# One flag of the framework: instructions ordered by its second machine model

## The chip, the cores and the metric

The kernel runs on one core of a Trainium2 chip. The core has five engines with an instruction stream each: TensorE (PE, matmuls, with the weight load shown apart as PEld), VectorE (DVE), ScalarE (ACT), GpSimd (POOL) and SyncE (SP, which issues most DMAs). An engine takes its instructions in the order in which the program has them; between engines, semaphores make an instruction wait for another's result. The metric is the time of one execution on the device in microseconds, the median of several runs.

## The reference

One inference step of a small decoder: two layers, a prompt group of 1024 tokens and a sample group of 8 sequences with one new token each, which share all weights. Layer 0 mixes with a gated linear recurrence (HGRN2), layer 1 with stick-breaking attention over one shared K/V; both layers also attend to 256 memory tokens, and both have a SwiGLU FFN. All inputs are float32.

```python
for l in range(DEPTH):
    hn = rmsnorm(h, g[0])
    if l < N_A:
        mix, S = a_mixer(hn, ...)          # HGRN2 recurrence and memory attention
    else:
        mix = b_mixer(hn, ...)             # stick-breaking over k_all, v_all and memory attention
    h = h + rmsnorm(mix, g[1])
    h = h + rmsnorm(swiglu(rmsnorm(h, g[2]), w_gu[l], w_down[l]), g[3])
    if l == N_A - 1:
        sb_k, sb_v = jnp.split(rmsnorm(h, g_kv) @ w_kv, 2, axis=-1)
```

For the sample group, attention reads caches: shared K/V in pages that a page table names (2 pages of 128 positions for each of the 8 sequences), and memory K/V of 256 tokens for each layer and sequence.

## The kernel before, in words

Tokens are on the free axis, features on the partitions. The prompt is cut into two groups of 512 tokens; group 1 carries the 8 sample tokens too, so its tiles are 520 wide and its matmuls go in two pieces of 260 columns, those of group 0 in one of 512.

**Projections.** All large products go through `proj` (L255 to L268). `split_w` loads 4 blocks of 128 x 128 weights in one DMA on SP's queue (L245), ScalarE rounds them to the fast float32 format of TensorE (L250), and VectorE forms the rest (L251); activations are split the same way (L271, L272). Each block then takes three matmuls (L264): high by high, high by low, low by high. The sums go into one of two PSUM accumulators (`mmp`, 2 buffers, tag `mm`); a third tile can start only when one has been evacuated (L403 on VectorE for the down projection, L281 and L474 for the FFN's gate and up, and others).

**Streams that are woven.** The kernel is written as generators; `weave` takes turns between streams in the order in which the program is written. Near the end it reads:

```python
weave((chain(b1.sb(), b1.mem()), 40), (chain(f0.part(0), f0.part(1)), 18))
weave((chain(b1.sb_sample(), b1.mem_sample()), 40), (chain(f0.part(2), f0.part(3)), 16))
o1 = out_proj(1, 1, A, True)
drain(o1.mm(b1.xo))
```

So layer 1's stick-breaking (`sb_prompt`, L1048 to L1075) and memory attention (`mem_attn`, L632 to L663) of the second group are written between the parts 0 and 1 of the first group's FFN, the sample group's two attentions between the parts 2 and 3, and the output projection behind both.

**The sample group's attention.** `sample_scores` puts the query in rows (transposes L679, copy L681), stores it to DRAM (L683) and loads it for each sequence to all partitions (L689). Then for each of 8 sequences it takes a tile of keys, 128 x 2 x 512, multiplies by the query (L690) and sums (L691), both on VectorE. `sample_pv` weights a tile of values (L702, in place), adds its two halves (L703), and TensorE sums over the partitions (L704); L707, L710, L271 and L272 put the result into the tiles `xo` that the output projection reads. The tiles `c` come from a pool of 4 buffers: in stick-breaking by gathers on POOL's queue (L731, two for each sequence), in memory attention by plain DMAs on SP's (L719). Between scores and weighting stand, in stick-breaking, L1084, a softplus (L1024 to L1027), three small matmuls (L1088 to L1090) and L1091, and in memory attention transposes (L745), a softmax (L747 to L752) and transposes back (L755).

**What sets the order.** The code above is only traced: the framework's `TileContext` collects the instructions with their dependences and priorities (the order written), and when the context closes, a scheduler plays them on a model of the machine. An instruction whose inputs are there and whose engine is free in the model is sent out, the earliest written first; the order in which they were sent is the order of each engine's stream, and is fixed. Buffers of a pool are handed out in the same run. A few copies are written for any engine (`nc.any.tensor_copy`, L777 and in `store_y`), and the scheduler picks the engine. The flag of the change stands in the last lines of `kernel`, where the context is opened.

Lines used below beside these: L293 to L295 (sum of squares over the partitions, and the reciprocal root), L304 (adding up squares), L310 (the normed residual), L384 to L390 (the residual itself), L846 and L849 (the recurrence for the sample group), L999 (evacuation of the shared K/V projection), L775 (transposes of the v projection).

## Time and profile before

| what | us |
|---|---|
| median of 3 runs | 2555.13 (2554.44 to 2561.5) |
| the profiled execution | 2559.18 |
| its span, first to last instruction | 2557.5 |
| TensorE busy in it | 2526.6 |
| mean granted TensorE clock in it | 0.992 |

The profile shows one execution. Rows of groups give line, engine, operation, output and inputs, shapes and count; behind the first bar the busy time of all in us and the mean of one in ns, behind the second the idle time of the engine just before them and what ended it. Rows of the timeline begin with the start in us and the duration, then engine, line and operation; a wait before the instruction stands in square brackets with what ended it. Matmuls of one run are merged into one row; a matmul in plain float32 can show as two records. Numbers of buffers are left out of the names.

### The profile page before, as it was taken

The numbers are of one execution on the slowest core, as the hardware profiler recorded it, in microseconds if no ns is written. First come the engines' busy times: TensorE is split into PE (matmuls) and PEld (weight loads), VectorE is DVE, ScalarE is ACT, GpSimd is POOL, SyncE is SP. The second block draws the span as 40 slices with busy tenths as digits, with TensorE's granted clock in tenths as the row PEclk, the third lists the DMA queues.
The fourth block names the chain that finished last, engine by engine and source line by source line (L and its number), as shares of the span: only waits on it lengthen the run. The fifth ranks groups of instructions, "written<-read, shape, count | busy, mean of one in ns | idle before, by whom it ended". The sixth has DMA issues, their size and how long they took to land.

```text
span 2557.5 us, 40523 instructions
## 1 busy us (share of the span) xinstructions
PE 2526.6 (99%) x15649; PEld 2205.3 (86%) x15649; DVE 1555.5 (61%) x2709; ACT 1183.6 (46%) x2186; POOL 40.7 (2%) x59
## 2 busy tenths in 40 slices
PE   8999999999999999999999999999999999999998
PEld 6888898888867888999999989867776798999998
DVE  6666566654675576555544576666678758444445
ACT  6346543243434455555433454566543245443334
POOL 1000000000000000000000000000021000000000
PEclk9999999998999999999999999999999999999999
DMA  6352242233563445322333446322157544333332
GB/s 183 110 161 71 73 150 77 65 111 110 158 182 91 128 153 178 103 86 60 97 94 92 125 146 189 113 82 75 46 175 217 156 125 125 111 88 100 95 92 67
DMA packets 457708, 297.91 MB, mean 116 GB/s; under 512 B 17573, under 2 KB 422642, under 8 KB 457514
## 3 DMA queue, kind: packets, MB, share of 16 engines
q1 hardware_dynamic: 454954, 286.92, 37.4%
q0 software_dynamic: 2560, 8.39, 1.1%
q8 instruction: 123, 2.02, 0.3%
q14 instruction: 71, 0.58, 0.1%
HBM read 265.44 MB, written 29.80 MB: 115 GB/s over the span
## 4 chain that ended last, share of the span: by engine, by line
issue 25%; PE 22%; DVE 1%; POOL 1%; DMA 1%; ACT 0%; DVEq 0%; POOLq 0%; SPq 0%; ACTq 0%
PE mm L264 21%; POOL c L731 1%; PE s L704 0%; DMA w<-in_w_gu 0%; DMA b<-qd 0%; DMA c<-in_cache_sb_v,pidx 0%; PE s L1125 0%; DVE c L690 0%; DVE sc L691 0%; PE ns L293 0%; PE s L440 0%; DVE yT L542 0%; DVE c L702 0%; PE s L508 0%; DVE yT L539 0%
## 5 line engine op out<-in xcount | busy, mean ns | idle before, releaser
L264 PE MATMUL mm<-x,ws 128*128 128x260 f32 (+1 forms) x10080 | 1676.5, 324 | 6.0 <-DVE ws L251 3.1
L264 PEld LDWEIGHTS mm<-x,ws 128*128 128x128 f32 x10080 | 1452.6, 189 | 167.4 <-issue 24.6
L250 ACT CAST ws<-w 128x512 fp32r<-128x512 f32 (+1 forms) x800 | 475.6, 595 | 911.9 <-PE mm L264 816.7
L251 DVE TENSOR_TENSOR ws<-w,ws 128x512 fp32r<-128x512 f32 (+1 forms) x800 | 522.2, 658 | 346.6 <-ACT ws L250 336.7
L264 PE MATMUL mm<-m,ws 128*128 128x260 f32 (+1 forms) x3168 | 542.6, 325 | 1.1 <-DVE t L474 0.5
L264 PEld LDWEIGHTS mm<-m,ws 128*128 128x128 f32 x3168 | 453.4, 188 | 59.8 <-issue 15.3
L403 DVE TENSOR_TENSOR r<-r,mm 128x520 f32<-128x520 f32 (+1 forms) x128 | 88.3, 690 | 88.9 <-PE mm L264 87.8
L281 DVE TENSOR_SCALAR t<-mm 128x512 f32<-128x512 f32 (+1 forms) x104 | 72.2, 694 | 110.2 <-PE mm L264 109.0
L474 DVE TENSOR_TENSOR t<-t,mm 128x512 f32<-128x512 f32 (+1 forms) x88 | 60.8, 691 | 116.1 <-PE mm L264 116.0
L285 DVE TENSOR_TENSOR t<-t,t 128x512 f32<-128x512 f32 (+1 forms) x88 | 61.1, 695 | 84.9 <-ACT t L284 84.8
L304 DVE TENSOR_TENSOR st<-st,n 128x512 f32<-128x512 f32 (+1 forms) x98 | 67.1, 691 | 6.9 <-ACT n L303 5.0
L272 DVE TENSOR_TENSOR m<-t,m 128x512 fp32r<-128x512 f32 (+1 forms) x88 | 61.0, 693 | 3.5 <-ACT m L271 1.6
L282 ACT ACTIVATE t<-t 128x512 f32<-128x512 f32 (+1 forms) x88 | 55.9, 635 | 12.1 <-DVE t L281 4.6
L271 ACT CAST m<-t 128x512 fp32r<-128x512 f32 (+1 forms) x88 | 54.9, 623 | 13.9 <-DVE t L474 6.9
L283 ACT ACTIVATE t<-t 128x512 f32<-128x512 f32 (+1 forms) x88 | 55.9, 635 | 2.6
L284 ACT ACTIVATE t<-t 128x512 f32<-128x512 f32 (+1 forms) x88 | 55.9, 635 | 2.3
L892 PEld LDWEIGHTS s<-a,a 128*128 128x128 f32 x448 | 53.4, 192 | 1.2
L892 PE MATMUL s<-a,a 128*128 128x64 f32 x448 | 53.1, 271 | 0.0
L731 POOL DMA_INDIRECT c<-in_cache_sb_k,pidx x16 | 16.6, 1038 | 1874.7 <-DVE r L403 1247.9
L1027 DVE SCALAR_TENSOR_TENSOR b<-b,b 128x512 f32<-128x512 f32 (+3 forms) x48 | 26.8, 558 | 29.7 <-ACT b L1026 29.3
L643 ACT ACTIVATE b<-s,nmx 128x256 f32<-128x256 f32 x64 | 29.8, 470 | 28.7 <-DVE nmx L637 28.7
L1075 PE MATMUL s<-b,a 128*128 128x512 f32 (+3 forms) x96 | 41.5, 514 | 0.3
(293 smaller groups left out, 1948.0 us busy)
## 6 DMA issues: line engine op xcount, KB each, us to landing
w<-in_w_gu SPq DMA_DIRECT2D x352, 256.0 KB
w<-in_w_down SPq DMA_DIRECT2D x160, 256.0 KB
w<-in_w_in_a SPq DMA_DIRECT2D x80, 256.0 KB
w<-in_w_o SPq DMA_DIRECT2D x64, 256.0 KB
w<-in_w_mem_kv SPq DMA_DIRECT2D x32, 256.0 KB
c<-in_cache_mem_k SPq DMA_DIRECT2D x16, 512.0 KB
c<-in_cache_mem_v SPq DMA_DIRECT2D x16, 512.0 KB
w<-in_w_kv SPq DMA_DIRECT2D x32, 256.0 KB
```

Source lines behind the costliest of these rows:

```text
L250: nc.scalar.copy(ws[:, 0, :n, :], raw[:, :n, :])
L251: nc.vector.tensor_sub(ws[:, 1, :n, :], raw[:, :n, :], ws[:, 0, :n, :].bitcast(F32))
L264: nc.tensor.matmul(ps[:, a, : PW[g]], wt, xt[k][:, xi, o : o + PW[g]], start=(k == 0 and wi == 0), stop=(k == nk - 1 and wi == 2),)
L272: nc.vector.tensor_sub(dst[1], src, dst[0].bitcast(F32))
L281: nc.vector.tensor_scalar(sv(x, g), pv(ps, g), -44.0, None, op0=ALU.max)
L282: nc.scalar.activation(d, x[:, :n], AF.Exp, scale=-1.0)
L283: nc.scalar.activation(d, d, AF.Ln, bias=1.0)
L285: nc.vector.tensor_mul(d, d, x[:, :n])
L304: nc.vector.tensor_add(acc[:, :n], acc[:, :n], t[:, :n])
L403: nc.vector.tensor_add(dst, dst, pv(ps, g))
L474: nc.vector.tensor_mul(sv(sg, g), sv(sg, g), pv(pu, g))
L892: nc.tensor.matmul(plv[:, hh, c, :], K_[:, hh, cs], rhs, start=True, stop=True)
```

## The change

The context is opened with the flag `schedule_with_timeline_sim`: the scheduler plays the instructions on the framework's second machine model, one of device occupancy, in place of its first. Nothing of the traced program changes: the same operations, tiles, pools and dependences go in.

```diff
--- before.py
+++ after.py
@@ -1221,7 +1221,7 @@
         args.append(nc.dram_tensor(f"in_{name}", a.shape, mybir.dt.from_np(a.dtype), kind="ExternalInput").ap())
     for name, shape in _OUTS:
         args.append(nc.dram_tensor(f"out_{name}", shape, F32, kind="ExternalOutput").ap())
-    with tile.TileContext(nc) as tc:
+    with tile.TileContext(nc, schedule_with_timeline_sim=True) as tc:
         tile_decoder(tc, *args)
     r = run_bass_kernel_spmd(nc, [arrays], core_ids=[0])
     return tuple(r.results[0][f"out_{name}"] for name, _ in _OUTS)
```

In the built program each engine has the same number of matmuls, vector operations and DMAs as before, but for seven of the copies for any engine, which are now on ScalarE and were on VectorE, and some 40 more instructions that only wait. The order differs on all engines. Around the sample group's attention in layer 1, TensorE's stream now reads (buffer numbers kept):

```
L264 Matmult mm_19059<-m_18847,ws_19056 128x512 x3
L264 Matmult mm_19088<-x_15705,ws_19080 128x260
L264 Matmult mm_19149<-x_15705,ws_19141 128x260
L1088 Matmult s_18243<-ss_18238,trif 128x32
L1089 Matmult s_18243<-ss_18238,ones 128x32
L1090 Matmult s_18243<-ss_18238,trif 128x32
L704 Matmult s_18249<-c_18250,sel 8x512
...
L704 Matmult s_18249<-c_18406,sel 8x512
L710 Matmult s_18452<-ident,b_18450 128x8 x4
L679 Matmult s_18469<-ident,ss_18466 8x128 x4
L264 Matmult mm_19088<-x_15705,ws_19080 128x260 x2
...
L745 Matmult s_18850<-ident,sc_18465 32x128 x2
L755 Matmult s_18860<-ident,b_18856 128x32 x2
L704 Matmult s_18865<-c_18866,sel 8x512
```

In the program before, matmuls of FFN parts 2 and 3 stood between all of these.

## The prediction

> **What bounds the kernel now.** I read the page's table of engines first, then the groups of instructions.
>
> ```profile
> span 2557.5 us, 40523 instructions
> PE 2526.6 (99%) x15649; PEld 2205.3 (86%) x15649; DVE 1555.5 (61%) x2709; ACT 1183.6 (46%) x2186; POOL 40.7 (2%) x59
> L264 PE MATMUL mm<-x,ws 128*128 128x260 f32 (+1 forms) x10080 | 1676.5, 324 | 6.0 <-DVE ws L251 3.1
> ```
>
> TensorE is the bound: outside its 2526.6 us it has 30.9 us in the whole span, and its largest group waited 6.0 us. No order of the same instructions can win much; an order can only lose the cover that the other engines' work now has. So I took the busy time of each engine by stage. Columns: stretch, length, busy time of PE, PEld, DVE, ACT, POOL (with counts), granted clock, DMA share, GB/s.
>
> ```profile
> 0.00:20.00 20.00, 9.98 (x32) 6.73 (x33) 11.41 (x32) 13.00 (x28) 7.29 (x27) 1.00 0.78 231
> 530.00:640.00 110.00, 110.00 (x506) 90.40 (x505) 56.11 (x89) 39.50 (x68) 0.00 (x0) 0.89 0.39 117
> 640.00:780.00 140.00, 137.56 (x594) 105.01 (x593) 95.48 (x139) 52.64 (x91) 0.00 (x0) 1.00 0.56 166
> 1600.00:1845.00 245.00, 244.32 (x1043) 177.28 (x1042) 158.94 (x295) 151.94 (x292) 0.00 (x0) 1.00 0.27 80
> 1885.00:2040.00 155.00, 148.94 (x611) 108.17 (x610) 128.04 (x178) 48.31 (x88) 26.52 (x26) 0.98 0.67 202
> 2160.00:2557.00 397.00, 388.87 (x3236) 385.82 (x3234) 192.56 (x295) 160.97 (x273) 0.00 (x0) 0.99 0.31 93
> ```
>
> Of the 30.9 us, 10.0 lie in the first 20 us, 8.1 in the last stretch, 6.1 in 1885 to 2040 and 2.4 in 640 to 780; 4.3 are left for all the rest. Stick-breaking for the second group (1600 to 1845), full of round trips between engines, idles 0.7 us. The stretch 1885 to 2040 is another matter: there the sample group's attention runs, DVE is busy for 128.0 of 155 us, and TensorE is nevertheless fed, because layer 1's FFN parts 2 and 3 are woven into it. That is the place to ask what another order does.
>
> **The change part by part.** No instruction is added or removed but a few waits, and seven copies that may run on either engine go from VectorE to ScalarE. What changes is the order on each engine, so I read the order of the built program, beside the old one. Three things stand in it.
>
> First, many transposes and round trips of TensorE stand later. The transposes of the v projection stand 20 matmuls behind the tile's last one instead of 4, and the steps of stick-breaking are spread over more FFN matmuls. By the rows above there is little to win: 4.3 us of idle, and 0.11 x 110 = 12.1 us that 530 to 640 loses to its clock, if the new order kept that stretch denser. I count a gain of 5, between 0 and 14 (the 16.4 less a little, since the instructions there stay the same).
>
> Second, and this decides: the sample group's attention loses its cover. The FFN parts 2 and 3 now all stand ahead of it, spread over stick-breaking and memory attention. In the new order of TensorE, after the last matmul of part 3, come two matmuls of the next output projection, then the three small matmuls of L1088 to L1090, which need all eight scores; all eight L704 in a row; four transposes each of L710 and L679; 48 matmuls of 260 columns; then L745, L755, again eight L704 and L710. In the order of DVE, the 16 passes of the first scores (L690, L691) stand together with only five others between them, then the weighting (L702, L703), then the second group's 16 passes and its weighting. The second group's query is formed (L681) only behind the first group's weighting. So two chains stand behind each other, in place of work woven through 155 us. Their prices:
>
> ```profile
> L691 DVE TENSOR_REDUCE sc<-c 128x8 f32<-128x1024 f32 x24 | 29.0, 1214 | 0.0
> L690 DVE TENSOR_TENSOR c<-c,b 128x1024 f32<-128x1024 f32 x24 | 28.7, 1222 | 0.8 <-DMA b<-qd 0.8
> L251 DVE TENSOR_TENSOR ws<-w,ws 128x512 fp32r<-128x512 f32 x736 | 504.0, 690 | 296.9 <-ACT ws L250 287.5 <-DMA w<-in_w_in_b 6.0
> 1919.95 0.21 DVE L1084 TENSOR_TENSOR sc<-sc,biass 128x64 f32<-128x64 f32 x1
> 1926.57 1.22 DVE L702 TENSOR_TENSOR c<-c,sc 128x1024 f32<-128x1024 f32 x1
> 1948.94 1.88 PE L704 MATMUL s<-c,sel 128*8 128x512 f32 x4
> 1957.51 0.68 DVE L681 COPY b<-s 8x512 f32<-8x512 f32 x1 [0.19 <-PE s L679]
> 1963.86 2.36 DVE L690 TENSOR_TENSOR c<-c,b 128x1024 f32<-128x1024 f32 x2 [0.20 <-DMA b<-qd]
> 2006.29 0.38 PE L745 MATMUL s<-ident,sc 128*32 128x128 f32 x2
> 2010.86 2.36 DVE L702 TENSOR_TENSOR c<-c,ss 128x1024 f32<-128x1024 f32 x2
> 2014.34 0.68 DVE L403 TENSOR_TENSOR r<-r,mm 128x512 f32<-128x512 f32 x1
> 2030.96 1.02 PE L704 MATMUL s<-c,sel 128*8 128x512 f32 x2
> 2032.03 0.68 DVE L707 COPY b<-s 8x512 f32<-8x512 f32 x1 [0.27 <-PE s L704]
> 2034.15 0.17 DVE L272 TENSOR_TENSOR x<-s,x 128x8 fp32r<-128x8 f32 x1 [0.84 <-ACT x L271]
> ```
>
> Two passes back to back take 2.36, so one takes 1.18. The first chain:
> - Scores: 16 x 1.18 + 5 x 0.69 = 22.3 us. They cannot start before the query has gone through DRAM, 1963.86 - 1957.51 = 6.35 us behind L681. Behind L681 TensorE still has 36 matmuls of 512 columns, 8.6 us (30 take 7.13, the row is below). So 2.2 us are covered: 20.1.
> - From the scores to the weighting: 1919.95 to 1926.57, 6.6 us with other vector work in it; bare I take 3.5, no less than 2.4.
> - Weighting: two tiles take 2014.34 - 2010.86 = 3.48, eight 13.9 by DVE alone. Before, the first chain needed 1926.57 to 1950.82, 24.2 us, with gathers behind four buffers. Four of the eight gathers can again start only when a weighted tile is used up; I take 20.
> - To the next matmul: L707 to L272, 2.1.
>
> Together 45.7 us. The second: 6.35 for the query; 16 x 1.18 + 2 x 0.69 = 20.3; L745 to L702 4.6; weighting between 13.9 and 21.1 (2010.86 to 2031.98), its loads being plain ones, 16; and 2.1. Together 49.4 us. TensorE's own work inside the 95.1 us: 16 L704 at 0.94 (1.88 for two), 15.0; the 48 matmuls, 6.0; the small ones about 1.5. It idles 95.1 - 22.5 = 72.6 us where it idled 6.1: **+66**. Bounds: only the vector passes, 2 x 18.9 + 2 x 13.9 - 2.2 - 22.5 - 6.1 = +35; every dear end (6.6, 24.2, 21.1) 107.5 - 22.5 - 6.1 = +79.
>
> ```profile
> 623.02 7.13 PE L264 MATMUL mm<-m,ws 128*128 128x512 f32 x30
> 1529.02 5.99 PE L264 MATMUL mm<-x,ws 128*128 128x260 f32 x48
> ```
>
> Third, the same in small: evacuations of TensorE's two accumulators stand behind runs of vector work, and TensorE can start its next tile only in an evacuated one.
> - Layer 0's memory scores for the sample group: 16 passes and 16 other vector instructions in one stretch, 18.9 + 11.0 = 29.9 us, with three evacuations (L281, L403) behind 2 to 4 passes each. TensorE has 16 matmuls of 260 columns and four tiles of 15 there, 2.0 + 14.3, and one tile in hand, 3.6. About 10 are left, less the 2.4 now: **+7**, between 0 and 13.
> - The two K/V projections (L999): two accumulators take turns on each new x tile, 6 matmuls or 1.4 us a tile, while DVE needs L310 and L272 for each:
>
> ```profile
> L310 DVE SCALAR_TENSOR_TENSOR m<-m,par,st 128x512 f32<-128x512 f32 (+1 forms) x24 | 17.1, 748 | 4.1 <-ACT st L295 4.1
> L272 DVE TENSOR_TENSOR x<-m,x 128x512 fp32r<-128x512 f32 (+1 forms) x24 | 15.6, 687 | 0.0
> L384 DVE SCALAR_TENSOR_TENSOR r<-r,par,st 128x512 f32<-128x512 f32 (+1 forms) x24 | 17.3, 748 | 2.9 <-ACT st L295 2.9
> ```
>
>  That is 1.44 us, so TensorE keeps step only if DVE does nothing else, and four weight halves (2.8 us) stand in between: **+3** each, +6, between 0 and 16.
> - At the start of the last FFN, eight L384 (6.0 us) stand ahead of the evacuation that TensorE's third tile waits for: **+5**, between 0 and 12.
>
> The **sum** against the profiled execution, 2559.2 us about its span of 2557.5: 2559.2 + 66 + 7 + 6 + 5 - 5 = 2638. That execution lies 4 us above the median of 2555.1, so I say 2635.
>
> **The rivals.**
> 1. The transfers pace it. The sample tiles are 32 of 0.5 MB and 16 query broadcasts of 0.25 MB, 21 MB, in 95 us instead of 155:
>
> ```profile
> 1905.20:1908.60 3.40, 3.40 (x10) 2.62 (x9) 2.77 (x4) 0.02 (x1) 0.99 (x2) 0.50 0.92 282
> 1983.70:1987.10 3.40, 3.37 (x8) 2.69 (x9) 3.40 (x5) 0.00 (x0) 0.00 (x0) 0.50 0.79 239
> 1981.49 0.70 PE L264 MATMUL mm<-x,ws 128*128 128x512 f32 x2 [1.79 <-DVE t L474]
> 1983.73 22.72 PE L264 MATMUL mm<-x,ws 128*128 128x512 f32 x92 [1.53 <-DVE ws L251]
> ```
>
>  At 282 GB/s, with 0.92 of the engines busy, a chain's eight score tiles and queries (6.3 MB) take 22 us, as long as the passes; at that stage's 202 GB/s they take 31, 9 more in each chain, and the weightings go to their dear ends (9 together): 2635 + 27, 2660. For it: 0.67 of the DMA engines are busy there now. Against it: up to four tiles can be loaded ahead.
> 2. The clock. After waits of 1.79 and 1.53 us the clock stood at 0.50 for 3.4 us, which costs 1.7 us each time. A dozen new clusters of waits, some outside the chains where TensorE is the bound again: up to +20, 2655. For it: these rows. Against it: inside the chains a slow clock hides behind DVE. [...]
> 3. Shorter: the small items come to nothing and the chains cost the middle of their bounds and less, 50 instead of 66: 2559.2 + 50 - 5 - 4 = 2600, and 2585 at the cheap end. For it: DVE is idle for 39% of the span and could absorb the small items. Against: the score passes need the query, which comes late.
> 4. Faster: the sample chains stay hidden and the looser round trips pay. It gives 2555 - 6 - 14 = 2535. It decides if TensorE has 73 us of independent matmuls behind the query; the order gives it 8.6 us there and 50 matmuls between the chains.
> 5. The option changes the lists but not the times, because each engine waits for the same data anyway: 2555. The order on TensorE differs in thousands of places, and the two chains are plainly bare.
>
> **How the numbers follow.** My forecast 0.45, transfers 0.17, clock 0.13, shorter 0.17, faster 0.05, no change 0.03. The range 2590 to 2685 leaves out rivals 4 and 5, the cheap end of 3 and the far ends of 1 and 2 together. About 0.3% (7.7 us) is what a measurement can tell from no change: faster 0.05, within 0.03, slower 0.92.
>
> **What would show it.** Right: in the new trace, from about 1900 to 2060 us, a stretch of some 95 us in which TensorE is busy for a quarter; the chain of waits goes through L690, L691, L702 and L703 there; DVE's score passes stand back to back; eight L704 follow each other at DVE's or the gathers' pace. L745 waits some 20 us for the scores. Small waits of TensorE on L281 and L403 near 600 to 640, on L272 at both K/V projections. Wrong: if TensorE is still above 95% busy in that stretch, or if most of the loss lies in stick-breaking, where I expect none, or if the gathers (POOL idle, DVE waiting for them) set most of the 95 us.

## The result and the profile after

The changed kernel takes 2660.34 us in the median of five runs (2655.84 to 2664.53), against 2555.13 before (2553.58 to 2561.5): ratio 1.0407, 95% interval 1.0392 to 1.0423. It is 105 us slower, where the prediction said 80 and its range ended at 2685. The profiled execution took 2656.33 us.

From the page of the changed kernel, the span, the engines, and TensorE's busy time in tenths in 40 equal slices of the span:

```profile
span 2654.6 us, 40566 instructions
PE 2518.9 (95%) x15649; PEld 2219.1 (84%) x15649; DVE 1555.6 (59%) x2702; ACT 1182.4 (45%) x2193; POOL 45.2 (2%) x59
PE   8999999999999998999999999999995499999998
```

TensorE does the same work: its busy time even fell by 7.7 us. Outside it the span now has 2654.6 - 2518.9 = 135.7 us, where it had 30.9: +104.8. Less the 7.7 this is the 97.1 us by which the two profiled spans differ; the medians differ by 105, because the profiled execution lay 4 us above its median before and 4 us below it now. Two slices of the 40 show where most of it is. By stage (length, then busy time of PE, PEld, DVE, ACT, POOL; granted clock, DMA share, GB/s), first after, then before:

```profile
0.00:2024.00 2024.00, 1975.04 (x11623) 1716.43 (x11623) 1217.05 (x2205) 956.80 (x1798) 15.67 (x35) 0.99 0.38 112
2024.00:2130.00 106.00, 37.24 (x105) 13.49 (x104) 72.81 (x86) 4.01 (x13) 29.51 (x24) 0.61 0.59 184
2130.00:2654.00 524.00, 506.63 (x3922) 489.19 (x3922) 265.79 (x412) 221.60 (x382) 0.00 (x0) 0.99 0.33 97
```

```profile
0.00:1885.00 1885.00, 1868.77 (x11083) 1605.23 (x11084) 1159.17 (x2119) 912.61 (x1720) 14.18 (x34) 0.99 0.38 114
2040.00:2557.00 517.00, 508.87 (x3958) 491.88 (x3956) 268.30 (x413) 222.69 (x378) 0.00 (x0) 0.99 0.34 100
```

The sample group's attention of layer 1 (2024 to 2130) leaves TensorE idle for 68.8 us where it was 6.1 (1885 to 2040 before): +62.7. Ahead of it stand 49.0 us instead of 16.2 (+32.8), behind it 17.4 instead of 8.1 (+9.3). What TensorE waited for, in the whole kernel (total us, times, longest):

```profile
PE s L704 <- DVE c L703: 25.3, 10, 5.6
PE s L745 <- DVE sc L691: 18.3, 1, 18.3
PE s L1088 <- DVE ss L1027: 16.5, 1, 16.5
PE mm L264 <- DVE r L403: 11.6, 13, 2.6
PE mm L264 <- DVE t L281: 8.3, 3, 4.6
```

The first three rows are the two sample chains and were 1.9, 0.3 and nothing before. TensorE's side of them, then VectorE's (start, us, engine, line, operation; the wait in brackets):

```profile
2020.51 3.59 PE L264 MATMUL mm<-m,ws 128*128 128x512 f32 x14
2046.76 0.61 PE L1088 MATMUL s<-ss,trif 128*128 128x32 f32 x2 [16.48 <-DVE ss L1027]
2103.34 0.61 PE L745 MATMUL s<-ident,sc 128*32 128x128 f32 x2 [18.28 <-DVE sc L691]
```

```profile
2015.36 0.67 DVE L681 COPY b<-s 8x512 f32<-8x512 f32 x1
2021.42 2.38 DVE L690 TENSOR_TENSOR c<-c,b 128x1024 f32<-128x1024 f32 x2 [2.32 <-DMA b<-qd]
2044.02 1.22 DVE L691 TENSOR_REDUCE sc<-c 128x8 f32<-128x1024 f32 x1
2048.80 2.36 DVE L702 TENSOR_TENSOR c<-c,sc 128x1024 f32<-128x1024 f32 x2 [0.32 <-ACT sc L1092]
2060.41 1.23 DVE L702 TENSOR_TENSOR c<-c,sc 128x1024 f32<-128x1024 f32 x1 [2.89 <-DMA c<-in_cache_sb_v,pidx]
2077.82 0.68 DVE L681 COPY b<-s 8x512 f32<-8x512 f32 x1 [0.18 <-PE s L679]
2083.39 2.37 DVE L690 TENSOR_TENSOR c<-c,b 128x1024 f32<-128x1024 f32 x2 [4.42 <-DMA b<-qd]
2100.95 2.34 DVE L691 TENSOR_REDUCE sc<-c 128x8 f32<-128x1024 f32 x2
2106.38 4.63 DVE L702 TENSOR_TENSOR c<-c,ss 128x1024 f32<-128x1024 f32 x4
2117.41 1.23 DVE L702 TENSOR_TENSOR c<-c,ss 128x1024 f32<-128x1024 f32 x1 [3.98 <-DMA c<-in_cache_mem_v]
2130.01 0.17 DVE L272 TENSOR_TENSOR x<-s,x 128x8 fp32r<-128x8 f32 x1 [0.76 <-ACT x L271]
```

The FFN's last matmuls end at 2024.1; from there to 2130.0 the chain is bare, 105.9 us, with little for TensorE in between. The order is as the prediction laid it out: query, scores, small step, weighting, tail, and the same again.

The smaller waits. Four of TensorE's rows, and the two VectorE rows that explain a pair of them:

```profile
654.06 8.73 PE L264 MATMUL mm<-m,ws 128*128 128x512 f32 x30 [3.52 <-DVE t L281]
1060.98 1.22 PE L1075 MATMUL s<-b,a 128*128 128x256 f32 x2 [3.20 <-DVE b L1030]
1541.59 3.70 PE L264 MATMUL mm<-x,ws 128*128 128x260 f32 x16 [1.75 <-DVE x L272]
2258.71 3.52 PE L264 MATMUL mm<-x,ws 128*128 128x260 f32 x15 [4.60 <-DVE t L281]
```

```profile
1055.27 5.45 DVE L310 SCALAR_TENSOR_TENSOR m<-m,par,st 128x520 f32<-128x520 f32 x8
2252.66 5.39 DVE L384 SCALAR_TENSOR_TENSOR r<-r,par,st 128x512 f32<-128x512 f32 x8 [1.36 <-ACT st L295]
```

Twice eight scalings stand in one row on VectorE, and behind them the one result that TensorE needs (L1030, L281). Adding up the gaps by place: K/V projections 3.5 and 5.8, start of the first stick-breaking 7.5, last FFN 6.8, layer 0's sample attention 7.7 (2.4 before), the first 20 us 12.9 (10.0 before), 112 to 120 us 1.9, 228 to 236 us 3.5, 314 to 319 us 2.9.

### The profile page after: what moved, and what is told of

It is laid out like the page before. It is cut to its first block, busy times and chain, and to the rows that moved or that the text cites. A ratio compares the mean times of both kernels' runs of the same rounds, so it can differ in the third digit from the quotient of the medians.

```text
span 2654.6 us, 40566 instructions
## 1 busy us (share of the span) xinstructions
PE 2518.9 (95%) x15649; PEld 2219.1 (84%) x15649; DVE 1555.6 (59%) x2702; ACT 1182.4 (45%) x2193; POOL 45.2 (2%) x59
## 4 chain that ended last, share of the span: by engine, by line
PE 63%; issue 29%; DVE 5%; DMA 2%; POOL 1%; ACT 1%; SPq 0%; POOLq 0%; DVEq 0%; ACTq 0%
PE mm L264 52%; PE s L892 1%; POOL c L731 1%; PE mm L608 1%; PE s L663 1%; PE s L632 1%; PE mm L581 1%; PE s L704 1%; DVE sc L691 0%; DVE c L702 0%; DVE c L690 0%; PE s L656 0%; DMA c<-in_cache_mem_k 0%; PE ns L293 0%; PE s L1075 0%
## 5 line engine op out<-in xcount | busy, mean ns | idle before, releaser
L264 PE MATMUL mm<-x,ws 128*128 128x260 f32 (+1 forms) x10080 | 1677.2, 324 | 26.5 <-DVE r L403 7.7
L264 PEld LDWEIGHTS mm<-x,ws 128*128 128x128 f32 x10080 | 1455.1, 190 | 191.2 <-issue 27.6
L264 PE MATMUL mm<-m,ws 128*128 128x260 f32 (+1 forms) x3168 | 532.4, 324 | 7.5 <-DVE r L403 3.9
L264 PEld LDWEIGHTS mm<-m,ws 128*128 128x128 f32 x3168 | 453.5, 188 | 62.8 <-issue 10.3
L281 DVE TENSOR_SCALAR t<-mm 128x512 f32<-128x512 f32 (+1 forms) x104 | 72.2, 694 | 118.9 <-PE mm L264 118.5
L272 DVE TENSOR_TENSOR m<-t,m 128x512 fp32r<-128x512 f32 (+1 forms) x88 | 61.1, 695 | 5.1 <-ACT m L271 2.7
L704 PE MATMUL s<-c,sel 128*8 128x512 f32 x48 | 32.0, 793 | 25.3 <-DVE c L703 25.3
L271 ACT CAST x<-s 128x512 fp32r<-128x512 f32 (+1 forms) x36 | 16.0, 443 | 87.0 <-PE s L710 52.9
```

What stands on the lines that cost most here:

```text
L264: nc.tensor.matmul(ps[:, a, : PW[g]], wt, xt[k][:, xi, o : o + PW[g]], start=(k == 0 and wi == 0), stop=(k == nk - 1 and wi == 2),)
L271: nc.scalar.copy(dst[0], src)
L272: nc.vector.tensor_sub(dst[1], src, dst[0].bitcast(F32))
L281: nc.vector.tensor_scalar(sv(x, g), pv(ps, g), -44.0, None, op0=ALU.max)
L704: nc.tensor.matmul(po[:NB, :], sel[:, b, :], vt[:, 0, :], start=(b == 0), stop=(b == NB - 1))
```

## The experiments

Each kernel was timed beside the kernel before, whose median lay between 2555.1 and 2556.4 each time, so medians are compared directly. In kernels with added lines, line numbers of the profile are shifted.

**1. Lost cover under the first model.** The writing alone puts all four FFN parts ahead of the sample attentions; the flag is off. (The FFN in question is that of the first group; the text below misnames it.)

```diff
-    weave((chain(b1.sb(), b1.mem()), 40), (chain(f0.part(0), f0.part(1)), 18))
-    weave((chain(b1.sb_sample(), b1.mem_sample()), 40), (chain(f0.part(2), f0.part(3)), 16))
+    weave((chain(b1.sb(), b1.mem()), 40), (chain(f0.part(0), f0.part(1), f0.part(2), f0.part(3)), 36))
+    drain(b1.sb_sample(), b1.mem_sample())
```

> The first machine model is kept, and the writing alone puts FFN parts 2 and 3 of layer 1's second group ahead of the sample attentions: TensorE's list then has the first query, the three small matmuls, eight L704, the second query, 48 matmuls and eight more L704 at the same places (10935 to 11064 of TensorE's matrix instructions, within 40) as the changed kernel has them. Theory A (the loss is the lost cover): of the changed kernel's 105 us about 74 lie in that stage (idle 68.8 us from 2024 to 2130 where 6.1 were, and some 11 us more busy time there at half clock), so 2555 + 74 = 2629, between 2615 and 2645, with one stretch of 65 to 70 us idle on TensorE. Rival B (the second model's order costs it all over the kernel, and the stage would be as slow in any order): 2555 to 2575.

Measured: 2637.99 (2633.02 to 2641.05), ratio 1.0323 [1.0305, 1.034], +82 us: theory A. Its stage, and two of TensorE's new waits:

```profile
1996.00:2121.00 125.00, 47.41 (x148) 19.97 (x148) 79.66 (x103) 9.65 (x32) 31.99 (x28) 0.63 0.54 166
PE s L1088 <- DVE ss L1027: 26.8, 1, 26.8
PE s L656 <- DVE b L649: 7.9, 5, 2.7
```

77.6 us are idle there, 8 more than the 65 to 70 expected, because the memory attention's tail (L656) is bare too and because fewer FFN matmuls are left behind the query. The loss of the stage needs no second model: whoever takes the FFN away from the sample attention pays this much.

**2. Sample attentions first, second model.**

```diff
-    weave((chain(b1.sb(), b1.mem()), 40), (chain(f0.part(0), f0.part(1)), 18))
-    weave((chain(b1.sb_sample(), b1.mem_sample()), 40), (chain(f0.part(2), f0.part(3)), 16))
+    weave((chain(b1.sb_sample(), b1.mem_sample()), 40), (chain(f0.part(0), f0.part(1)), 16))
+    weave((chain(b1.sb(), b1.mem()), 40), (chain(f0.part(2), f0.part(3)), 18))
```

> The second model is kept; the sample attentions are written into FFN parts 0 and 1, the stick-breaking into parts 2 and 3, so that some 690 matrix instructions of TensorE stand between the first query and the last transposes instead of 130. Theory A: the 74 us of the stage come back and the other 31 stay: 2660 - 74 = 2586, between 2575 and 2605. Rival B (the second model's order costs it all over): above 2640. Rival C (the model now runs the FFN ahead of the stick-breaking, which becomes bare in its place): 2610 to 2650, with TensorE's idle time in one stretch before 2100 us, at L264 and L1063 to L1075 lines.

Measured: 2646.97 (2644.16 to 2650.24), 1.0355 [1.0339, 1.037]: 13 us less than the changed kernel. Theory A is out. The time lies in the ranges of rivals B and C alike; what speaks for C is the new idle stretch that it named. The stage of the sample attentions, and that of the last steps of stick-breaking:

```profile
1660.00:1780.00 120.00, 100.97 (x409) 75.53 (x408) 86.06 (x121) 39.83 (x76) 28.51 (x23) 0.93 0.65 194
2030.00:2130.00 100.00, 71.76 (x264) 44.25 (x263) 48.89 (x99) 50.84 (x110) 0.00 (x0) 0.91 0.02 6
```

The sample attentions still idle TensorE for 19.0 us with FFN around them, and now the end of stick-breaking is bare and idles it for 28.2. The bareness has moved.

**3 and 4. The part left out, both models.**

```diff
+        if l == 1:
+            for h in range(H):
+                split_to((xo[H + h][:, 0, G : G + NB], xo[H + h][:, 1, G : G + NB]), qm[h // 2][:, h % 2, G : G + NB])
+            return
```

(and the same with `Qs` and `xo[h]` at the head of `sb_sample`).

> Layer 1's two sample attentions are left out (their eight token columns get a copy of the query), second model. Theory A: what is left of the difference to the next kernel is what the change costs outside that stage, 97 - 74 = 23 us, between 15 and 33; the time is near 2526 + 23 = 2549. Rival B: the difference to the next kernel stays at 70 us or more.

> The same part left out, first model. Both theories: the time before less TensorE's own work for that part (22.5 us by the prediction's count) and the 6.1 us it idled there: 2555 - 28.6 = 2526, between 2518 and 2534. If the sample attention also slowed its neighbours (DVE was busy for 128 of 155 us there), lower: down to 2510.

Measured: second model 2562.37 (2557.05 to 2566.68), first model 2521.53 (2520.29 to 2523.38); ratios to before 1.0026 [1.0013, 1.0038] and 0.9869 [0.9853, 0.9885]. The second model's page, then the first's:

```profile
span 2561.5 us, 40207 instructions
PE 2495.4 (97%) x15591; PEld 2220.0 (87%) x15591; DVE 1483.8 (58%) x2622; ACT 1180.3 (46%) x2188; POOL 7.1 (0%) x27
```

```profile
span 2518.4 us, 40196 instructions
PE 2493.3 (99%) x15591; PEld 2192.0 (87%) x15591; DVE 1489.5 (59%) x2629; ACT 1182.8 (47%) x2181; POOL 7.8 (0%) x27
```

Run 4 lies in its range. Without the stage the change costs 40.8 us, outside the ranges of theory A (15 to 33) and of rival B (70 or more): 41.0 by the time outside TensorE's busy time (66.1 against 25.1). The sample attention adds 97.9 us under the second model (2660.3 - 2562.4) and 34.6 under the first (2556.2 - 2521.5): 63 more, in line with the 62.7 of idle time read above. The 23 of theory A was 97 - 74: the 97 is the difference of the two profiled executions, where the medians differ by 105, and the 74 had added the slower matmuls inside the stage, which these runs do not bear out.

**5. Half of the sample tiles loaded.**

```diff
         def load(b):
+            if b >= 4:
+                return kept[b - 4]
             t = C()
+            kept.append(t)
```

(in both loaders; for plain loads in layer 1 only.)

> The changed kernel, but in layer 1's sample attentions only the first four tiles of each of the four rows of eight are loaded; the fifth to the eighth take the same four buffers again, already multiplied. VectorE's and TensorE's instructions and their order stay, half of the transfers are gone. In the changed kernel VectorE waited in the two weightings some 14 us for tiles (8.5 in the first, 5.0 in the second), and about 2 in the scores. Theory A (VectorE's passes pace most of the stage): 10 to 18 us less, 2642 to 2650, and the stage still idles TensorE for over 50 us. Rival 1 of the prediction (the transfers pace it): 27 us less or more, below 2633.

Measured: 2643.5 (2639.65 to 2646.39), 1.0342 [1.0328, 1.0357]: 16.8 us less, in the range of theory A. The transfers are a share of the stage, VectorE's passes and the round trips the rest: TensorE still idles 58.4 us there by its gaps.

**6. Both sample chains side by side.**

```diff
-    weave((chain(b1.sb_sample(), b1.mem_sample()), 40), (chain(f0.part(2), f0.part(3)), 16))
+    weave((b1.sb_sample(), 20), (b1.mem_sample(), 20), (chain(f0.part(2), f0.part(3)), 16))
```

> The changed kernel with layer 1's two sample attentions written side by side instead of one behind the other: both queries stand in front of the three small matmuls, and all sixteen L704 behind them. VectorE's passes stay, what goes is one chain's latency: a query through DRAM (4.9 us), L745 to L702 (3.1), a tail (4.5), and waits for tiles that the other chain's work can fill. Theory A: 12 to 30 us less, 2630 to 2648. Rival (four tile buffers shared by both chains hold up the loads, so nothing is won): 2655 or more.

Measured: 2653.57 (2653.17 to 2662.26), 1.0399 [1.0382, 1.0415]: 6.8 us less, between the two. TensorE's first wait shows why:

```profile
PE s L1088 <- DVE ss L1027: 43.1, 1, 43.1
```

All 32 score passes, 37.8 us at 1.18, now stand ahead of L1088. One chain's latency is saved, but TensorE has nothing between the chains either.

**7. FFN parts 2 and 3 held back.**

```diff
+                with tc.issue_after(held[7].ins) if late else nullcontext():
-                pg = proj(g, w_gu[l], 0, ND, (f0 + j) * P, self.xt)
+                    pg = proj(g, w_gu[l], 0, ND, (f0 + j) * P, self.xt)
```

(`held[7]` is the last transpose of layer 1's first sample query, `late` holds for parts 2 and 3 of the first group in layer 1; the same for `pu`. `issue_after` only sets the order within TensorE's list.)

> The changed kernel, with one thing forced: the gate and up matmuls of FFN parts 2 and 3 (first group, layer 1) stand behind the first sample query's transposes in TensorE's list. The model then keeps that query at matrix instruction 10395 (10428 before the change, 10935 with it) and spreads the chains over 670 instructions to 11064. Theory A (the loss of the stage is the lost cover, and the model spent it early): 63 to 74 us less, 2586 to 2600; the rest of the kernel keeps its 41 us (the difference of the two kernels without sample attention). Rival C (what the FFN parts covered ahead of it becomes bare): 2610 to 2645, with new idle time of TensorE between 1550 and 1950 us. Rival B (order does not matter there): 2655 or more.

Measured: 2649.62 (2647.29 to 2661.11), 1.0377 [1.0355, 1.0399]: 10.7 us less, between the ranges of rivals C and B; the profiled execution took 2659.58. The last steps of stick-breaking with the memory attention, the stage of the sample chains, and two of the last steps:

```profile
1860.00:1944.00 84.00, 58.92 (x159) 33.70 (x158) 37.49 (x81) 36.54 (x85) 1.89 (x2) 0.73 0.03 10
1944.00:2075.00 131.00, 113.99 (x454) 84.86 (x453) 96.33 (x129) 39.93 (x70) 33.89 (x26) 0.93 0.63 196
1886.99 1.13 PE L1080 MATMUL s<-b,a 128*128 128x512 f32 x2
1891.03 1.12 PE L1080 MATMUL s<-b,a 128*128 128x512 f32 x2
```

The sample chains are covered again (17.0 us idle instead of 68.8), but 25.1 us of idle time stand in the 84 us before, where no FFN matmul is left. In the whole kernel TensorE's idle time fell by 24.3 us (135.7 to 111.4), but the same 15649 records of matmuls kept it busy for 27.5 us longer (2546.4 against 2518.9): the granted clock was 0.73 and 0.93 in the two stretches. The lists say why cover is missing. Counted there, FFN matmuls (L264) between the first and the last of the 32 steps of stick-breaking:

| kernel | FFN matmuls between the 32 steps | a step |
|---|---|---|
| before | 631 | 20 |
| after | 949 | 31 |
| FFN held (7) | 661 in the first 22 intervals, then none | 30, then 0 |
| FFN rationed (9) | 567 | 18 |

A bare step takes 4.0 us (1886.99 to 1891.03, in a stretch at a clock of 0.73). Twenty matmuls of 512 columns last 4.8 us at the 0.238 us each of the prediction's rows, and before, stick-breaking idled TensorE for 0.7 us; so some ten of the 30 cover nothing. Over 22 steps these are by estimate 220 matmuls, 52 us of cover spent where it buys nothing.

**8. Side by side, first model.** The edit of 6 in the kernel before.

> The kernel before the change (first model) with the two sample attentions side by side, as a kernel that might beat both: the stage idled TensorE for 6.1 us, most of it at 1902 to 1904 and 1980 to 1984, so at most 6 us can be won: 2549 to 2556. If the shared tile buffers crowd, up to 10 us more: 2566.

Measured: 2561.28 (2557.8 to 2570.82), 1.0026 [1.0016, 1.0036]: 5 us slower than before, in the range that was given for crowded buffers. No kernel here that does the whole work beats the one before.

**9 and 10. FFN rationed, both models.** Every FFN tile of parts 0 to 3 is put behind an attention step of the written order (`held` collects the last matmul of each step):

```diff
+            def behind(lag):
+                return tc.issue_after(held[-lag]) if (g, l) == (0, 1) and pi < 4 else nullcontext()
...
+                with behind(3):
+                    pg = proj(g, w_gu[l], 0, ND, (f0 + j) * P, self.xt)
```

(2 for `pu`; 3 and 2 in turn for the down projection.)

> The changed kernel, with each FFN tile of parts 0 to 3 (first group, layer 1) forced behind the attention step two or three steps back in the written order, so that the model can't run the FFN ahead. Counted in TensorE's list, 631 matmuls of the FFN stand between the first and the last of the 32 steps of stick-breaking before the change (20 a step), 949 with it (31 a step), 661 in the first 22 steps and none in the rest with parts 2 and 3 held; here 567 (18 a step), and 500 are left for the sample attentions. Theory (the second model spends the FFN on stick-breaking's steps, each of which took 4.0 us bare and held 7 us of FFN, and what comes last is bare, whichever it is): about 63 us less than the changed kernel, 2597, between 2588 and 2610, with TensorE idle for under 20 us between 1550 and 2140. The 41 us of the rest stay. Rival D (the second model's order of VectorE inside the stage costs by itself, cover or not, as the 16 us of waits of the held kernel at 1964 to 2072 hint): 2615 to 2640.

> The same forced order in the kernel before the change (first model), as a control of what the forcing itself costs: its list has the same 20 matmuls a step and the same places of the sample chains. Both theories: 2556 to 2566. If it were over 2575, the run beside it could not be read.

Measured: second model 2649.53 (2648.32 to 2658.6), 1.0373 [1.0357, 1.0389]; first model 2575.59 (2569.67 to 2578.26), 1.008 [1.0066, 1.0094]. Run 9 lies above the ranges of its theory and of rival D. The control came out at the line that was drawn for it: forcing costs 19 us under the first model, so run 9 by itself can't be read. Beside its control it is 74 us slower, of which 41 lie outside the stage by runs 3 and 4; 33 are left in the stage, if forcing costs the same under both models, which is not known. The second model's kernel from 1700 us on, then the control's same part, from 1670 us on:

```profile
1700.00:1890.00 190.00, 174.66 (x672) 126.37 (x670) 115.08 (x215) 112.30 (x216) 0.00 (x0) 0.96 0.21 62
1890.00:1945.00 55.00, 49.12 (x217) 38.76 (x216) 26.57 (x56) 23.25 (x58) 4.11 (x4) 0.97 0.28 81
1945.00:2100.00 155.00, 133.19 (x517) 95.92 (x516) 113.68 (x155) 43.56 (x77) 29.25 (x24) 0.92 0.60 184
```

```profile
1670.00:1850.00 180.00, 171.96 (x663) 119.32 (x663) 113.83 (x215) 109.88 (x216) 0.00 (x0) 0.98 0.21 63
1850.00:2040.00 190.00, 176.60 (x743) 129.98 (x742) 145.06 (x214) 65.38 (x130) 40.73 (x28) 0.99 0.61 182
```

No stretch is bare any more; 15.3, 5.9 and 21.8 us of idle time lie in many waits of 0.7 to 6.4 us, in all three parts. The same 1406 records of matmuls take 400 us here and 370 in the control: 43.0 us of idle time against 21.4, and TensorE busy for 357.0 us against 348.6, at granted clocks of 0.92 to 0.97 against 0.98 and 0.99. So 30 of the 33 us are found, two thirds as waits and one third as busy time.

**11. Vector work in turns outside the stage.**

```diff
+            with turn(seen):
-            nc.vector.scalar_tensor_tensor(t[:, :n], R[k][:, :n], gc(k), rstd[:, :n], op0=ALU.mult, op1=ALU.mult)
+                nc.vector.scalar_tensor_tensor(t[:, :n], R[k][:, :n], gc(k), rstd[:, :n], op0=ALU.mult, op1=ALU.mult)
```

(`turn` puts it behind the last vector instruction of tile k-2, or of the norm before; the same in the residual.)

> The changed kernel, with one order forced on VectorE outside the sample stage: in the normalisations and in the residual, the scaling of tile k (L310, L384) stands behind the last vector instruction of tile k-2, and one normalisation behind the one written before it; so eight L310 or L384 no longer stand in a row. TensorE's waits at those places in the changed kernel are 3.5 us at 941 to 950, 7.5 at 1045 to 1061, 5.8 at 1524 to 1542 and 6.8 at 2199 to 2259, 23.6 together. Theory (runs of like vector work stand ahead of the one result that TensorE waits for): 10 to 20 us less than the changed kernel, 2640 to 2650. Rival (those waits are round trips that any order has): within 5 us, 2655 to 2665, or more where VectorE now waits for ScalarE.

Measured: 2645.69 (2643.07 to 2654.28), 1.0361 [1.0339, 1.0382]: 14.7 us less than the changed kernel, in the range of the theory. The four places idle 14.1 us instead of 23.6, so runs of vector work caused 9.5 us of these waits; the other 5 us of the gain were not traced.

**12. Sample passes in turn, on top of 9.**

```diff
+            with tc.issue_after(evac[-1]):
-            nc.vector.tensor_mul(kt, kt, qb.unsqueeze(1).to_broadcast([P, 2, 512]))
+                nc.vector.tensor_mul(kt, kt, qb.unsqueeze(1).to_broadcast([P, 2, 512]))
```

(and for L691, L702, L703; `evac[-1]` is the vector instruction that emptied the last FFN tile written.)

> The kernel with the FFN rationed under the second model (2649.5 us), and on top of it each pair of passes of the sample chains (L690 and L691, L702 and L703) forced behind the evacuation of the FFN tile written just before it, so that no four weightings and four halvings stand in a row as they did at 2083 to 2090. In the rationed kernel TensorE waited for VectorE 6.4 us at 1965, 2.6 at 2041, 3.5 at 2056 and 6.4 at 2082, each followed by 3 to 7 us at half clock. Rival D of that run (the second model's order of VectorE inside the stage costs by itself): 2625 to 2640. If it is not that but the placing of TensorE's own instructions: 2645 or more.

Measured: 2650.04 (2645.95 to 2654.24), 1.0372 [1.0354, 1.039]: no gain over 9. Two of TensorE's waits (L704 has become L719 here):

```profile
1999.29 1.88 PE L719 MATMUL s<-c,sel 128*8 128x512 f32 x2 [5.39 <-DVE c L718]
2093.73 1.87 PE L719 MATMUL s<-c,sel 128*8 128x512 f32 x2 [4.44 <-DVE c L718]
```

The waits for evacuations have gone over into waits for the weighted tiles. Rival D is not borne out: breaking up the runs of passes on VectorE won nothing.

## Why the prediction was right, and where it was not

**The main step held.** It said that the sample group's attention would lose its cover and cost 66 us. The stage idles TensorE 62.7 us more, the kernels without it put it at 63, and taking the cover away without the flag costs 82 (run 1). The parts of the chains, forecast and measured between the same points (the query from the start of L681, the weighting to the end of the last L704, the tail from L707 to L272):

| part | first chain: said, was | second chain: said, was |
|---|---|---|
| query through DRAM | 6.35, 6.1 | 6.35, 5.6 |
| scores | 22.3, 23.8 | 20.3, 19.9 |
| to the weighting | 3.5, 3.6 | 4.6, 3.1 |
| weighting | 20, 26.7 | 16, 22.2 |
| tail | 2.1, 1.6 | 2.1, 1.4 |
| covered by TensorE at the start | 8.6, 8.7 | - |

The bare time is 105.9 us, forecast 95.1. Both weightings were too cheap, and came out beyond even their dear ends, 24.2 and 21.1. VectorE waited for value tiles there, 8.5 us in the first chain and 4.7 in the second, and GpSimd held gathers back for 4.1 us until an L704 had used up an earlier tile, there being four buffers. At a clock of 0.50 one L704 (two records) took 1.88 us (from 2053.29), at 1.00 it took 1.02 (from 2062.42), where 0.94 was counted. The idle time is nevertheless smaller than the 72.6 forecast, because TensorE's own work in it, slowed by the same clock (0.61 over the stage), was 37.2 us and not 22.5. That the 66 lies so near to the 63 is in part luck: 10.8 us too little bare time and 14.7 us too little work of TensorE in it nearly cancel.

**The small items were mis-sized.** The three places named were there: layer 0's memory scores 7 forecast, 5.3 more than before measured (at 650 to 670 us, not at 600 to 640); K/V projections 6 and 9.3; last FFN 5 and 6.8. Together 18 against 21.4. What the sum lacked were 18.7 us of places not listed: the start of the first stick-breaking (7.5), the ends of two chains at 228 and 314 us (6.4), the start of the kernel (2.9) and 112 us (1.9). The first of them is the very mechanism that was priced for the last FFN, eight scalings in a row ahead of one result that TensorE needs. It was read in the order for one FFN and not looked for elsewhere. Run 11 breaks such runs up, and the start of the first stick-breaking then idles about 4 us instead of 7.5. The places at 112, 228 and 314 us and the start of the kernel are read from the trace and not tested.

**The gain of 5 did not come.** It rested on 12.1 us that 530 to 640 us lost to the clock. But the kernels of runs 1 and 4, whose TensorE list is the same up to far behind that stretch, lost less there without any change of order; run 4's row:

```profile
530.00:640.00 110.00, 110.00 (x550) 90.30 (x550) 60.12 (x97) 43.08 (x76) 0.00 (x0) 0.97 0.41 121
```

A clock of 0.97 against 0.89, and 550 matmuls in place of 506 in the same 110 us. It was one execution's luck, and had been read as a price of the order. It is also why TensorE's busy time could fall by 7.7 us in the changed kernel's profile, which has 0.97 there too. The other source, looser round trips, was worth nothing either, as stick-breaking idled 0.7 us before.

**Sum.** 66 + 7 + 6 + 5 - 5 = 79 against 105: 63 for the stage, 41 for the rest where 13 stood. The range held it; the forecast was 25 us short, all of it in the small items and the gain.

**The rivals.** Transfers: 2660 was its figure, and the time came out there, but not by it. With half of the tile loads gone 16.8 us are saved (run 5), where that rival asked for 27 or more. Clock: up to +20 was its price. Outside the chains it comes to some 2 us at most: TensorE's busy time without the stage was 2495.4 under the second model and 2493.3 under the first, at mean clocks of 0.985 and 0.997, and these two executions also differ at 530 to 640 us, 0.91 against 0.97. The two waits that the prediction quotes for it, 1.79 and 1.53 us, stand ahead of one and the same slow stretch (1983.70 to 1987.10, at 0.50), so they are one fall of the clock and not two. Faster, no change and shorter are out.

**Why giving the cover back did not help.** That it would was expected in these experiments and fell (runs 2, 7, 9). The second model does not only put the FFN in another place; it lays 31 FFN matmuls at each step of stick-breaking where 20 fill it. The prediction saw the steps spread over more matmuls and counted this as a small chance of gain. By the counts it is where the cover goes: the FFN is used up early, and whatever comes last is bare, the sample chains as written, stick-breaking's end where the FFN is held or the sample written first. That a better ration would win the 63 us back under the second model is not shown: run 9 rations the FFN and, beside the 41 us outside the stage, stays 33 us behind its control. Most of this remainder is found, 21.6 us of short waits and 8.4 us of longer busy time at a lower clock, but its cause is open; VectorE's runs of passes are not it (run 12), and whether the places of TensorE's small matmuls are was not tried.

## What to carry to other kernels

Where one engine is the bound, count its independent work between the steps of each latency-bound chain, in the built order, before and after: cover beyond what a step needs is spent for nothing and is missing under the chain that comes last (here 31 FFN matmuls a step where 20 had been enough, and 68.8 us idle under the sample chains). When one run of like instructions ahead of a waited-for result is found, look for the same shape at every other place before the sum is closed. And do not price a clock loss from a single execution: compare two with the same order first (here 0.89 in one and 0.97 in the other over the same 110 us).

## What the runs showed of the hardware

In the changed kernel's trace the granted clock stood at 0.50 for 3.4 us (from 1541.8, from 2258.6) or longer (6.8 us from 1528.1, 34.1 from 2026.5), and one fall came behind 3.4 us in which TensorE was busy for 1.65. Two stretches of 3.4 us, each with the one behind it (length, then TensorE's busy time; the granted clock is the third number from the end):

```profile
1538.40:1541.80 3.40, 1.65 (x12) 1.33 (x11) 3.40 (x6) 1.27 (x3) 0.00 (x0) 1.00 0.32 95
1541.80:1545.20 3.40, 3.40 (x17) 3.40 (x17) 3.06 (x5) 0.62 (x1) 0.00 (x0) 0.50 0.22 64
2197.10:2200.50 3.40, 2.01 (x9) 1.31 (x7) 3.40 (x7) 1.26 (x2) 0.00 (x0) 1.00 0.37 111
2200.50:2203.90 3.40, 2.64 (x12) 2.19 (x13) 3.40 (x7) 3.32 (x6) 0.00 (x0) 1.00 0.53 154
```

With 1.65 us busy the next stretch is at 0.50, with 2.01 it stays at 1.00. This gives no threshold: the stretch from 2060.57 to 2063.98, 1.63 us busy, was followed by one at 1.00 as well. A wait of 1.75 us (until 1541.59) stood ahead of a fall in the one place, and one of 2.15 (until 2201.26) did not in the other; the first lies inside one of the stretches, the second across two. Why the clock fell at the first place and not at the second is not shown.
